# A two-layer decoder step on one Trainium2 core: input sums moved to GpSimd, one top-k search done by bits, output weights split earlier, modulation steps placed later

## The chip, the cores and the metric

The kernel runs as one program on one core of a Trainium2 chip. The core has a matrix engine (TensorE, PE in the rows), VectorE (DVE), ScalarE (ACT), GpSimd (POOL) and SyncE (SP), which issues nearly all the DMAs. The metric is the device time of one execution in microseconds, lower is better. The kernel before takes 2554.56 us, the median of three runs (2552.93 to 2556.01).

## The reference, cut to what matters

The model has two layers, 1024 prompt tokens and 8 sample tokens, a width of 1024, everything in float32. Each sub-layer modulates its input by a shift and a scale that come from a conditioning vector (adaLN), mixes, and ends with `LayerNorm(ALPHA*x + (1+gate)*y)`.

- The modulation of a layer is `silu(c) @ w_ada + b_ada`, cut into six parts of 1024: shift, scale and gate of the mixer, then shift, scale and gate of the channel mixer.
- Layer 0 mixes with a spatial gating unit (SGU): `z = gelu(h @ w_in + b_in)`, halves u and v, v normalised and mixed over chunks of 128 tokens, then `(u * mixed) @ w_out`.
- Layer 1 mixes with sparse attention: an indexer scores all keys for each query, the top 256 of them (128 for a sample token) are kept, and softmax attention runs over those.
- Both layers end with a ConvGLU: `a, u = split(h @ w_up)`, a causal depthwise convolution of width 3 over a, and `(gelu(conv) * u) @ w_down`, with 2816 inner columns.

## The kernel before, in words

**Numbers and tiles.** Activations lie transposed: 128 features on the partitions, tokens along the row, in three chunks of 384, 384 and 264 tokens. Every float32 operand of a large product is split into a high part and a rest (`split`, L111: the high part is a rounded copy, the rest a subtraction, L118), and each product is three matmuls (`mm3`, L98). A piece of weights is 512 KB: SP loads it into one of three `raw` buffers, then its high part (`whi`, L115) and its rest (`wlo`, L118) are written by the engines that `eng` names, GpSimd for both in most places, into tiles of a pool: `W` (4 buffers), `T` (13), `P` (2) or `E` (2).

**The order of the work.** The text of the program gives a priority. A planner then places the instructions of every engine by its own estimate of durations and by the free buffers, and each engine runs in the order that came out. In the loop over the last 18 of 22 ConvGLU tiles (`seven_tile`, L855) the order of TensorE is pinned to that of the text. A queue `fq` holds small steps of other work; `pump(n)` emits the next n of them between two products.

**The SGU stage (up to about 400 us).** `zload(i)` (L341) fetches piece i: 0 to 7 for v, 8 to 15 for u, 16 to 23 the columns of `sgu_w_out`. The loop over u (L630) computes one piece per turn for three chunks, multiplies u into the mixed v (`product`, L626), and in its last turn splits the products into the operand `Hh`, `Hl`. Each turn loads the piece two turns ahead; pieces 18 to 23 are loaded after the loop. `ada_round(0, 2, rawmk)` (L245) is queued after turn 11: eight steps of two 512 KB loads of `w_ada` into `raw` buffers and four matmuls, and an end that turns the sums into shift, scale and gate of the channel mixer. After the loop `gates` and `affine` (L360) prepare the small vectors, and `out_proj` (L669) multiplies: chunk by chunk, for eight pieces, `dense` (L168) and then `accumulate` (L657; L661 on VectorE adds the product into R). Behind each chunk the steps of its LayerNorm (`ln_steps`, L431) are queued: three that normalise (their row tiles come from the pools that `tags` names), and eight that write the next operand with the vectors of `affine`.

**The ConvGLU (about 400 to 1145 us and 1790 to 2500 us).** Inner columns are tiles of 128. Tiles 0 to 3 run in full; from tile `S0` = 4 on, Strassen's scheme does a tile in seven half products. That scheme needs sums of parts of the input (`form_steps`, L781): `sums(k)` makes three rows t1, t2, t4 for each of four k, `parts_of` splits them into tiles `F`, and `third(k)` writes a difference of parts back into `Hh`, `Hl` after tile 3 has used them. These twelve steps are emitted one by one during tiles 2 and 3. The products of the second half (`down`, L709) are queued in `dq` and go to PSUM and then, by L661, into R. In layer 0 each Strassen tile also emits one step of the next layer's modulation (`slow`, L904).

**The top-k search (about 1280 to 1565 us).** For each block of 128 queries the 256th largest score is found bit by bit (`search`, L1216): 31 rounds, in each of which one pass counts the scores above a candidate (L1229 on VectorE) and a few one-column instructions update the candidate. The plan (L39) has VectorE search blocks 2 and 4 together, then block 7 alone (`V2`); ScalarE does the others. The rounds are spread between the heads of the attention.

Of the kernel before, what the change touches and what calls it, by code (L numbers as in the profile page):

```python
# [10 lines left out]
I32 = mybir.dt.int32  # L11
BF = mybir.dt.bfloat16
AF = mybir.ActivationFunctionType
OP = mybir.AluOpType
# [6 lines left out]
T = NPT + NB  # L21
# [31 lines left out]
S0 = 4  # L53
# [7 lines left out]
def hybrid_step(  # L61
# [95 lines left out]
    fq = deque()  # L157

    def pump(n=1):
        for _ in range(n):  # L160
            if fq:
                fq.popleft()()
# [131 lines left out]
    R = newR("R")  # L294
# [44 lines left out]
    pieces = {}  # L339

    def zload(i):  # L341
        if i < 16:
            m = zorder[i]
            pieces[i] = load_w(win[:, m * 128:(m + 1) * 128], 128, eng="AV" if i < 2 else "GG")
        elif i < 24:
            dt = i - 16
            pieces[i] = load_w(sgu_w_out[0][:, dt * 128:(dt + 1) * 128], 128, pool=[None, None, "T", "T", "T", "T", "T", "T"][dt])

# [281 lines left out]
    for i in range(8, 16):  # L630
        m = i - 8
# [11 lines left out]
        if i == 11:  # L643
            drain()
            for c in range(3):
                for k in range(4):
                    product(k, c)
            fq.extend(ada_round(0, 2, rawmk))
        zload(i + 2)
    drain()  # L650
    for i in range(18, 24):
        zload(i)
# [16 lines left out]
    def out_proj(pcs, R, gate, af):  # L669
        for c in range(3):  # L670
            for dt in range(8):
                b = dense(pcs[dt], 128, c)
                accumulate(R, dt, c, b, gate)
                pump(2)
            fq.extend(ln_steps(R, c, af))

    af = affine(0, 3, 0)
    out_proj([pieces[16 + d] for d in range(8)], R, gate, af)


    def conv_glu(l, R, gate, tail_af, last, slow, prefetch=None):
# [99 lines left out]
        def form_steps():  # L781
# [5 lines left out]
            def sums(k):  # L787
# [5 lines left out]
                V.tensor_tensor(t1, t1, x11[1], op=OP.subtract)  # L793
                V.tensor_tensor(t2, x22[0], t1, op=OP.subtract)
                V.tensor_tensor(t2, t2, x22[1], op=OP.add)
                G.tensor_tensor(t4, x21[0], t2, op=OP.subtract)
# [6 lines left out]
            def third(k):  # L803
                x12, x22 = X(0, 1, k), X(1, 1, k)
                d = sm.tile([128, 384], F32, name="d", tag="ht", bufs=2)[:, :TH]
                V.tensor_tensor(d, x22[0], x12[0], op=OP.subtract)
                V.tensor_tensor(d, d, x22[1], op=OP.add)
                V.tensor_tensor(d, d, x12[1], op=OP.subtract)
                split(Hh[:, k, TH:2 * TH], Hl[:, k, TH:2 * TH], d, "A", "V")
# [45 lines left out]
        def seven_tile(ff):  # L855
# [47 lines left out]
            operand(ff, "S4")  # L903
            times = slow.popleft()(True) if slow else None  # L904

# [142 lines left out]
    xsp = [dram.tile([128, KT, CH[c][1]], F32, name=f"xsp{c}") for c in range(3)]  # L1048
    af_box = {}

    spilled = []

    def spill(c):
        SP.dma_start(xsp[c], R[c])
        spilled.append(c)

    class Lazy:
        def __iter__(self):
            if "v" not in af_box:
                af_box["v"] = affine(1, 0, 1)  # L1060
            return iter(af_box["v"])

# [9 lines left out]

    conv_glu(0, R, gate, Lazy(), spill, slow, lambda: (dload(0), dload(1)))

# [141 lines left out]
    def search(name, items, eng):  # L1216
# [9 lines left out]
        if eng == "V":  # L1226
            def counts(c):
                for i, (_, x, n, W, K) in enumerate(items):
# [15 lines left out]
            V.tensor_tensor(cand, cand, bit(30), op=OP.bitwise_or)  # L1244
            V.tensor_scalar(acc, s, 2.0, None, op0=OP.add)
            V.tensor_tensor(tab, pows.unsqueeze(2).to_broadcast([128, 31, m]), acc.unsqueeze(1).to_broadcast([128, 31, m]),
                            op=OP.mult)
            V.tensor_scalar(tab[:, 0, :], tab[:, 0, :], -0.5, None, op0=OP.add)
            V.tensor_scalar(sg, s, 2.0, None, op0=OP.mult)
            for i in range(30, -1, -1):  # L1250
                yield counts(cand)
# [533 lines left out]
```

## Time and profile before

| | |
|---|---|
| median of three runs | 2554.56 us (2552.93 to 2556.01) |
| the profiled execution's own time | 2547.5 us |
| its span, first to last instruction | 2545.8 us |
| TensorE busy in the span | 2450.0 us |
| VectorE / GpSimd / ScalarE busy | 1741.6 / 1376.0 / 985.9 us |
| mean granted TensorE clock | 0.983 |

The profile is of one execution. TensorE is busy for nearly all of the span, so the places to read are those where it waits, and those where its granted clock is below 1. The clock column is in parts of full speed, so a stretch of n us at 0.95 has lost 0.05 n of full-speed time.

### The profile page before, as it was taken

How to read it: one execution, taken by the hardware profiler on the slowest of the kernel's cores; microseconds unless marked ns; L12 is line 12 of the kernel's file. 1: busy time of each engine (PE TensorE's matmuls, PEld its weight loads, DVE VectorE, ACT ScalarE, POOL GpSimd, SP SyncE). 2: the span in 40 equal slices, each digit the busy share in tenths (PEclk: the TensorE clock that was granted, in tenths of full speed). 3: DMA queues.
4: the chain of work that ended last, by engine and by line, in shares of the span. 5: the costliest groups of instructions: out<-in, count | busy, mean ns of one | idle time of the engine just before them, and what ended most of it. 6: DMA issues, size and time to landing. Idle time of an engine off the chain costs nothing.

```text
span 2545.8 us, 41058 instructions
## 1 busy us (share of the span) xinstructions
PE 2450.0 (96%) x15552; PEld 2299.4 (90%) x15552; DVE 1741.6 (68%) x3872; ACT 985.9 (39%) x1906; POOL 1376.0 (54%) x1406
## 2 busy tenths in 40 slices
PE   7999999999999999999999989898999999999997
PEld 5898799789999999998987988777999999999997
DVE  4224335777777777865798997434688888888867
ACT  3121224123333333344567876542423333333341
POOL 3333525436666666574345766533635666666675
PEclk8999999999999999999999999999999999999998
DMA  8413402422222222211114211234111111111112
GB/s 282 124 55 108 125 17 72 131 64 83 81 77 61 81 83 83 82 49 52 62 35 113 54 54 64 63 117 120 59 42 42 50 50 50 47 48 49 50 56 80
DMA packets 203980, 192.14 MB, mean 75 GB/s; under 512 B 9806, under 2 KB 178246, under 8 KB 202999
## 3 DMA queue, kind: packets, MB, share of 16 engines
q1 hardware_dynamic: 200582, 179.86, 22.9%
q0 software_dynamic: 2688, 9.44, 1.2%
q8 instruction: 123, 2.02, 0.3%
q14 instruction: 74, 0.61, 0.1%
q10 hardware_dynamic: 513, 0.23, 0.0%
HBM read 178.41 MB, written 11.27 MB: 75 GB/s over the span
## 4 chain that ended last, share of the span: by engine, by line
PE 78%; DVE 11%; POOL 3%; ACT 3%; issue 2%; DMA 2%; POOLq 0%; SPq 0%; DVEq 0%; ACTq 0%
PE psA L852 28%; PE psB L96 23%; PE psA L96 20%; PE psB L197 3%; PE psB L260 2%; DVE junk L1229 2%; DVE R L661 1%; PE psA L197 1%; DVE S L1209 1%; ACT junk L1260 1%; DMA raw<-in_dsa_w_out_dram 1%; DVE Cc L753 1%; ACT Hh L392 0%; DMA adaw<-in_w_ada_dram 0%; DVE L L1534 0%
## 5 line engine op out<-in xcount | busy, mean ns | idle before, releaser
L661 DVE SCALAR_TENSOR_TENSOR R<-psB,g,R 128x384 f32<-128x384 f32 (+1 forms) x976 | 528.9, 566 | 182.5 <-PE psB L96 181.8
L852 PE MATMUL psA<-Hh,ws 128*128 128x344 f32 x2304 | 578.0, 320 | 0.0
L852 PEld LDWEIGHTS psA<-Hh,ws 128*128 128x128 f32 x2304 | 403.5, 188 | 12.6 <-issue 12.6
L96 PE MATMUL psA<-Hh,whi 128*128 128x384 f32 (+1 forms) x1168 | 381.7, 328 | 13.6 <-POOL whi L115 8.2
L96 PE MATMUL psA<-Hh,wlo 128*128 128x384 f32 (+1 forms) x1168 | 378.6, 325 | 1.2 <-DVE wlo L118 1.2
L96 PE MATMUL psA<-Hl,whi 128*128 128x384 f32 (+1 forms) x1168 | 379.1, 325 | 0.3 <-POOL Hl L398 0.3
L852 PE MATMUL psA<-Hl,ws 128*128 128x344 f32 x1152 | 367.6, 319 | 0.0
L96 PE MATMUL psB<-gh,whi 128*128 128x384 f32 (+1 forms) x1056 | 342.1, 324 | 9.5 <-DVE R L661 7.5
L96 PE MATMUL psB<-gl,whi 128*128 128x384 f32 (+1 forms) x1056 | 338.8, 321 | 0.1
L96 PE MATMUL psB<-gh,wlo 128*128 128x384 f32 (+1 forms) x1056 | 337.2, 320 | 1.4 <-POOL wlo L118 1.4
L118 POOL TENSOR_TENSOR ws<-raw,ws 128x512 fp32r<-128x512 f32 x152 | 201.4, 1327 | 240.1 <-ACT ws L113 240.1
L118 POOL TENSOR_TENSOR wlo<-raw,whi 128x1024 fp32r<-128x1024 f32 (+1 forms) x91 | 232.8, 2560 | 66.7 <-ACT gh L113 48.4
L96 PEld LDWEIGHTS psA<-Hh,whi 128*128 128x128 f32 x1168 | 223.2, 191 | 35.7 <-issue 12.5
L96 PEld LDWEIGHTS psA<-Hl,whi 128*128 128x128 f32 x1168 | 223.2, 191 | 9.8 <-issue 8.6
L96 PEld LDWEIGHTS psA<-Hh,wlo 128*128 128x128 f32 x1168 | 222.9, 191 | 10.0 <-issue 6.7
L118 POOL TENSOR_TENSOR ws<-sf,ws 128x512 fp32r<-128x512 f32 x136 | 176.3, 1302 | 85.5 <-ACT ws L113 74.6
L852 PE MATMUL psA<-F,ws 128*128 128x344 f32 x1296 | 221.9, 320 | 0.0
L852 PEld LDWEIGHTS psA<-Hl,ws 128*128 128x128 f32 x1152 | 216.2, 188 | 0.0
L96 PEld LDWEIGHTS psB<-gh,whi 128*128 128x128 f32 x1056 | 199.0, 188 | 18.1 <-DVE R L661 11.7
L852 PEld LDWEIGHTS psA<-F,ws 128*128 128x128 f32 x1296 | 207.8, 188 | 0.0
L96 PEld LDWEIGHTS psB<-gh,wlo 128*128 128x128 f32 x1056 | 198.9, 188 | 1.7 <-POOL wlo L118 1.7
L96 PEld LDWEIGHTS psB<-gl,whi 128*128 128x128 f32 x1056 | 199.1, 189 | 0.8 <-DVE gl L118 0.8
(419 smaller groups left out, 4730.1 us busy)
## 6 DMA issues: line engine op xcount, KB each, us to landing
raw<-in_ffn_w_up_dram SPq DMA_DIRECT2D x88, 512.0 KB
raw<-in_w_ada_dram SPq DMA_DIRECT2D x64, 512.0 KB
raw<-in_ffn_w_down_dram SPq DMA_DIRECT2D x44, 512.0 KB
adaw<-in_w_ada_dram SPq DMA_DIRECT2D x32, 512.0 KB
raw<-in_sgu_w_in_dram SPq DMA_DIRECT2D x16, 512.0 KB
raw<-in_dsa_w_in_dram SPq DMA_DIRECT2D x16, 512.0 KB
raw<-in_dsa_w_out_dram SPq DMA_DIRECT2D x32, 256.0 KB
raw<-in_sgu_w_out_dram SPq DMA_DIRECT2D x8, 512.0 KB
```

The lines of the kernel that those rows point to most:

```text
L96: pinned(PE.matmul(out, l, r, start=start, stop=stop))
L118: (V if e_lo == "V" else G).tensor_tensor(lo, src, f(hi), op=OP.subtract)
L197: PE.transpose(out, in_, ident[:in_.shape[0], :in_.shape[0]])
L260: pinned(PE.matmul(st["b"][32 * g:32 * g + 32, :512], SCT[:, k, :], rw[g // 2][:, (g % 2) * 512:(g % 2 + 1) * 512], start=(k == 0), stop=( ...
L661: V.scalar_tensor_tensor(R[c][:, dt, :npr], b[:, :npr], gp[:, dt:dt + 1], R[c][:, dt, :npr], op0=OP.mult, op1=OP.add)
L753: V.scalar_tensor_tensor(Cc[:, a0:c0 + npr], As[:, a0 - d:c0 + npr - d], w, Cc[:, a0:c0 + npr], op0=OP.mult, op1=OP.add)
L852: pinned(PE.matmul(b[:, :TH], w[i][:, k, :], x[j], start=first and k == 0 and n == 0, stop=last and k == 3 and n == 2, skip_group_check=True))
L1209: V.scalar_tensor_tensor(S(b)[:, s:s + n], rl[:, :n], WI[:, b, h:h + 1], S(b)[:, s:s + n], op0=OP.mult, op1=OP.add)
L1229: V.tensor_scalar(junkV[:n, :W], x, c if c == 0.0 else f(c[:n, i:i + 1]), 0.0, op0=OP.is_ge, op1=OP.add, accum_out=cnt[:n, i:i + 1])
L1260: A.activation(junkA[:n, :W], x, AF.Sign, bias=c if c == 0.0 else f(c[:n, i:i + 1]), scale=scale if scale == -1.0 else scale[:n, i:i + 1], ...
```

## The change

- **Output pieces of the SGU.** Pieces 16 and 17 are loaded after turns 11 and 12 of the loop over u, piece 18 after turn 14. Piece 16 goes to pool `T`, piece 17 to `E`, piece 18 to `W`; pieces 19 to 23 stay behind the loop and in `T`.
- **Modulation, first seam.** `ada_round(0, 2)` is queued just before `out_proj`; its nine steps go out at one per product from the fifth of chunk 0, then two per product. `affine(0, 3, 0)` is made when its vectors are first used (`Lazy`). The row tiles of the LayerNorm of chunks 0 and 1 come from `P`.
- **Modulation, second seam.** The first Strassen tile of layer 0 emits no step of the next layer's modulation; the rest follow one tile later each.
- **Input sums.** In `sums` the two instructions that make t2, and in `third` all three, run on GpSimd in place of VectorE: 20 instructions in each layer.
- **Search.** The search of block 7 alone keeps a table of bit patterns; a round has two one-column instructions behind the count in place of three.

```diff
@@ zload
-            pieces[i] = load_w(..., 128, pool=[None, None, "T", "T", "T", "T", "T", "T"][dt])
+            pieces[i] = load_w(..., 128, pool=["T", "E", None, "T", "T", "T", "T", "T"][dt])
@@ loop over u
                     product(k, c)
-            fq.extend(ada_round(0, 2, rawmk))
-        zload(i + 2)
+        if i < 14:
+            zload(i + 2)
+        if i in (11, 12, 14):
+            zload({11: 16, 12: 17, 14: 18}[i])
     drain()
-    for i in range(18, 24):
+    for i in range(19, 24):
         zload(i)
@@ out_proj
                 accumulate(R, dt, c, b, gate)
-                pump(2)
-            fq.extend(ln_steps(R, c, af))
-
-    af = affine(0, 3, 0)
-    out_proj([pieces[16 + d] for d in range(8)], R, gate, af)
+                pump(2 if c else int(dt > 3))
+            fq.extend(ln_steps(R, c, af, tags="PP" if c < 2 else "EP"))
+
+    class Lazy:
+        def __init__(self, *args):
+            self.args, self.v = args, None
+        def __iter__(self):
+            if self.v is None:
+                self.v = affine(*self.args)
+            return iter(self.v)
+
+    fq.extend(ada_round(0, 2, rawmk))
+    out_proj([pieces[16 + d] for d in range(8)], R, gate, Lazy(0, 3, 0))
@@ form_steps: sums
-                V.tensor_tensor(t2, x22[0], t1, op=OP.subtract)
-                V.tensor_tensor(t2, t2, x22[1], op=OP.add)
+                G.tensor_tensor(t2, x22[0], t1, op=OP.subtract)
+                G.tensor_tensor(t2, t2, x22[1], op=OP.add)
@@ form_steps: third
-                V.tensor_tensor(d, x22[0], x12[0], op=OP.subtract)
-                V.tensor_tensor(d, d, x22[1], op=OP.add)
-                V.tensor_tensor(d, d, x12[1], op=OP.subtract)
+                G.tensor_tensor(d, x22[0], x12[0], op=OP.subtract)
+                G.tensor_tensor(d, d, x22[1], op=OP.add)
+                G.tensor_tensor(d, d, x12[1], op=OP.subtract)
@@ seven_tile
-            times = slow.popleft()(True) if slow else None
+            times = slow.popleft()(True) if slow and ff > S0 else None
@@ search
+            if m == 1:
+                tab = tab[:, :, 0].bitcast(I32)
+                V.tensor_scalar(bs, cnt, K - 0.5, -1.0, op0=OP.is_ge, op1=OP.mult)
+                V.tensor_tensor(tab, bits, bs.to_broadcast([128, 31]), op=OP.bitwise_and)
+                V.tensor_tensor(tab[:, 1:31], tab[:, 1:31], bits[:, 0:30], op=OP.bitwise_xor)
+                for i in range(30, -1, -1):
+                    yield counts(cand)
+                    V.tensor_scalar(bs, cnt, K - 0.5, float(1 << i), op0=OP.is_gt, op1=OP.mult)
+                    V.scalar_tensor_tensor(cand, bs, tab[:, i:i + 1], cand, op0=OP.bitwise_xor, op1=OP.bitwise_xor)
+            else:
...
-            for i in range(30, -1, -1):
+            for i in range(30, -1, -1) if m > 1 else ():
                 yield counts(cand)
                 V.scalar_tensor_tensor(acc, cnt, K - 0.5, sg, op0=OP.is_gt, op1=OP.mult)
                 V.scalar_tensor_tensor(bs, acc, -0.5 * (1 << i), tab[:, i, :], op0=OP.mult, op1=OP.add)
```

## Rows read from the trace of the kernel before

**Rows 1.** The page's busy times (us, share of the span, instructions) by engine.

```profile
PE 2450.0 (96%) x15552; PEld 2299.4 (90%) x15552; DVE 1741.6 (68%) x3872; ACT 985.9 (39%) x1906; POOL 1376.0 (54%) x1406
```

**Rows 2.** The page's chain that ended last, shares of the span by engine.

```profile
PE 78%; DVE 11%; POOL 3%; ACT 3%; issue 2%; DMA 2%; POOLq 0%; SPq 0%; DVEq 0%; ACTq 0%
```

**Rows 3.** Busy time by stretch: length, engines (instructions), granted clock, DMA share, GB/s.

```profile
289.00:304.00 15.00, 9.65 (x45) 9.33 (x44) 8.21 (x17) 3.17 (x9) 15.00 (x6) 0.77 0.21 62
310.00:398.00 88.00, 88.00 (x597) 87.77 (x596) 28.41 (x58) 24.08 (x39) 34.63 (x41) 1.00 0.09 25
534.00:570.00 36.00, 31.75 (x184) 28.59 (x184) 33.04 (x73) 10.75 (x21) 16.15 (x11) 0.95 0.20 61
573.00:1139.00 566.00, 565.22 (x3596) 547.44 (x3595) 434.18 (x890) 198.13 (x370) 357.46 (x260) 1.00 0.26 77
1387.00:1521.00 134.00, 124.49 (x809) 119.61 (x808) 128.91 (x379) 109.44 (x264) 87.59 (x212) 0.95 0.19 54
1845.00:1892.00 47.00, 42.12 (x248) 40.61 (x247) 46.09 (x84) 11.31 (x23) 19.42 (x15) 0.96 0.12 36
```

**Rows 4.** Timeline of TensorE, 295 to 304 us: start, duration, instruction, idle before.

```profile
299.14 0.69 PE L96 MATMUL psA<-Hh,whi 128*128 128x384 f32 x1 [5.35 <-POOL whi L115]
...
301.23 0.52 PE L96 MATMUL psA<-Hl,whi 128*128 128x384 f32 x1
...
303.67 0.34 PE L96 MATMUL psA<-Hh,whi 128*128 128x384 f32 x1
303.84 0.34 PE L96 MATMUL psA<-Hl,whi 128*128 128x384 f32 x1
```

**Rows 5.** Timeline of GpSimd, 276 to 318 us: the splits of the output pieces.

```profile
288.37 8.52 POOL L118 TENSOR_TENSOR wlo<-raw,whi 128x1024 fp32r<-128x1024 f32 x1
296.86 2.23 POOL L115 TENSOR_SCALAR whi<-raw 128x1024 fp32r<-128x1024 f32 x2
...
314.23 1.05 POOL L115 TENSOR_SCALAR whi<-raw 128x1024 fp32r<-128x1024 f32 x1
315.36 2.42 POOL L118 TENSOR_TENSOR wlo<-raw,whi 128x1024 fp32r<-128x1024 f32 x1
```

**Rows 6.** Timeline of SP's DMA queue, 250 to 320 us.

```profile
261.64 8.66 SPq L252 DMA_DIRECT2D raw<-in_w_ada_dram  x4
274.41 33.26 SPq L124 DMA_DIRECT2D raw<-in_sgu_w_out_dram  x8
```

**Rows 7.** The modulation's line L260: duration ns min/median/max, first and last start.

```profile
L260 PE MATMUL psB<-raw,SCT x256: 592/605/617, 230.3 to 1074.5; 128*32 128x512 f32 x128
```

**Rows 8.** TensorE's waits in 534 to 570 us, then in 1845 to 1892 us.

```profile
PE psB L96 <- DVE R L661: 3.6, 3, 3.0
...
PE psB L96 <- DVE R L661: 3.5, 3, 2.0
```

**Rows 9.** VectorE's groups, 534 to 570 us by form: busy us, mean ns.

```profile
L808 DVE TENSOR_TENSOR d<-d,Hl 128x344 f32<-128x344 f32 x2 | 1.8, 883 | 0.0
...
L806 DVE TENSOR_TENSOR d<-Hh 128x344 f32<-128x344 f32 x2 | 0.9, 502 | 0.0
```

**Rows 10.** VectorE's groups in 1845 to 1892 us, the same columns.

```profile
L661 DVE SCALAR_TENSOR_TENSOR R<-psB,g,R 128x384 f32<-128x384 f32 (+1 forms) x31 | 17.1, 570 | 0.0
...
L793 DVE TENSOR_TENSOR raw<-raw,Hl 128x344 f32<-128x344 f32 x4 | 4.9, 1236 | 0.0
...
L795 DVE TENSOR_TENSOR raw<-raw,Hl 128x344 f32<-128x344 f32 x4 | 2.5, 628 | 0.0
```

**Rows 11.** Line L797, the last sum of an input on GpSimd, both layers.

```profile
L797 POOL TENSOR_TENSOR raw<-raw,Hl x8: 922/962/1287, 469.8 to 1892.5; 128x344 f32<-128x344 f32 x8
```

**Rows 12.** VectorE's groups in 1380 to 1620 us: the search's one-column instructions.

```profile
L1252 DVE SCALAR_TENSOR_TENSOR boxV<-boxV 128x1 f32<-128x1 f32 (+1 forms) x41 | 11.0, 269 | 0.2
L1253 DVE SCALAR_TENSOR_TENSOR boxV<-boxV,misc 128x1 int32<-128x1 f32 x31 | 10.3, 333 | 0.2
L1254 DVE TENSOR_TENSOR boxV<-boxV 128x1 int32<-128x1 int32 (+1 forms) x41 | 10.0, 251 | 0.5
```

More of the change, by code (lines that the diff above doesn't have):

```diff
@@ L346, in zload @@
             dt = i - 16
-            pieces[i] = load_w(sgu_w_out[0][:, dt * 128:(dt + 1) * 128], 128, pool=[None, None, "T", "T", "T", "T", "T", "T"][dt])
+            pieces[i] = load_w(sgu_w_out[0][:, dt * 128:(dt + 1) * 128], 128, pool=["T", "E", None, "T", "T", "T", "T", "T"][dt])
     def mod(L, i):
@@ L1048, in hybrid_step @@
     xsp = [dram.tile([128, KT, CH[c][1]], F32, name=f"xsp{c}") for c in range(3)]
-    af_box = {}
     spilled = []
@@ L1055, in spill @@
         spilled.append(c)
[L1057 to L1061, printed above, removed]
     dwin = dsa_w_in[0]
@@ L1071, in dload @@
             pcs[i] = load_w(dwin[:, o:o + n], n, [None, None, "T", "T", "P"][i] if i < 5 else None, eng=QE if i >= 9 else "GG")
-    conv_glu(0, R, gate, Lazy(), spill, slow, lambda: (dload(0), dload(1)))
+    conv_glu(0, R, gate, Lazy(1, 0, 1), spill, slow, lambda: (dload(0), dload(1)))
     misc = Tt("misc")
@@ L1244, in search @@
             V.tensor_tensor(cand, cand, bit(30), op=OP.bitwise_or)
[L1245 to L1249, printed above, removed]
-            for i in range(30, -1, -1):
+            if m == 1:
[8 more added lines that the diff above has]
+            else:
+                V.tensor_scalar(acc, s, 2.0, None, op0=OP.add)
+                V.tensor_tensor(tab, pows.unsqueeze(2).to_broadcast([128, 31, m]), acc.unsqueeze(1).to_broadcast([128, 31, m]),
+                                op=OP.mult)
+                V.tensor_scalar(tab[:, 0, :], tab[:, 0, :], -0.5, None, op0=OP.add)
+                V.tensor_scalar(sg, s, 2.0, None, op0=OP.mult)
+            for i in range(30, -1, -1) if m > 1 else ():
                 yield counts(cand)
```

## The prediction

> **What bounds the kernel now.** I read the busy times of the page first: TensorE works 2450.0 us of the 2545.8 us span, VectorE 1741.6 [rows 1]. The chain of waits says the same: 78% of it is TensorE, and VectorE comes next with 11% [rows 2]. So time can only come from where TensorE idles or runs at a lower clock, and the busy times by stretch show where the change touches such a place [rows 3]: 289 to 304 us, where the SGU's output projection begins; 534 to 570 and 1845 to 1892 us, where the ConvGLUs of the two layers make the Strassen inputs; 1387 to 1521 us, where block 7 is searched beside the attention. In the last three VectorE is busy 33.0 of 36, 46.1 of 47 and 128.9 of 134 us: there it is VectorE that sets the pace.
>
> **Part 1, the output pieces.** Between 289 and 304 us TensorE idles 15 - 9.65 = 5.35 us, all of it before 299.14, where it waits for a high part from GpSimd [rows 3, 4]. GpSimd was held up: one rest took 8.52 us where a later one takes 2.42, and the next high parts start at 296.86 [rows 5]. All eight pieces are fetched only from 274.41 on, behind the 16 loads of the modulation, the last four of which go out from 261.64 [rows 6]. Piece 17 has moreover to wait for buffers of `W`: four, two per piece, held by pieces 14 and 15 until their products are done. After the wait the matmuls run at the lower clock level (1.2 of 2.4 GHz), with 0.52 in place of 0.34 us each; the 14 from 299.14 to 303.67 take 4.53 us, and at 0.17 from start to start would take 2.4 [rows 4]: 2.1 us lost. With pieces 16 to 18 split during the loop over u, the first three products (24 matmuls of 0.17, 4.1 us each) are covered. The other five pieces cost GpSimd 1.05 + 2.42 = 3.5 us each [rows 5], less than a product, and have 12 us of lead, minus what the last v tiles take to leave pool `T`. I count **-5.35 - 2.1 = -7.5 us**; worth nothing if piece 19 is late instead.
>
> **Part 2, the modulation in the output projection.** Nothing is added or dropped: eight steps of two loads and four matmuls (L260, 0.6 us each [rows 7]), one end with a copy, four transposes and four sums, and the ten small instructions of `affine` move behind the start of the projection. On SP its 16 loads now stand behind the output pieces, ahead of the ConvGLU's first weights. At 8.66 / 4 = 2.2 us each [rows 6] they take 35 us, from about 17 us into the projection (five pieces at 3.5 us must leave the `raw` buffers first): done some 52 us in. The projection takes about 109 us (289 to 398, without a gap from 310 on [rows 3]), so over 50 us are left for the LayerNorm steps of two chunks and the first weights. I count 0; without that cover each us of lateness is a us. Chunk 0's and 1's row tiles both in `P` cost nothing either: chunk 1's steps stand behind chunk 0's in the queue.
> The step left out of the first Strassen tile is also 0: from 573 to 1139 us TensorE works 565.2 of 566 us [rows 3], each later step goes out one tile later, and the last matmul of them at 1074.5 [rows 7] leaves room for one more tile.
>
> **Part 3, the input sums.** Per layer 8 instructions of `sums` and 12 of `third` go from VectorE to GpSimd. A sum of this shape takes 0.50 us on VectorE where nothing disturbs it [rows 9] and 0.96 on GpSimd [rows 11]. Layer 0: TensorE idles 36 - 31.75 = 4.2 us, 3.6 of it for VectorE's additions into R, the longest 3.0 [rows 3, 8], and loses 0.05 x 36 = 1.8 us to the clock. Two of the four `third` run in that stretch: 0.9 + 0.9 + 1.8 = 3.6 us [rows 9], L807, which has no row, at the price of L806. Gain between -6.0 (all of idle and clock) and, if VectorE is blocked for all the six instructions' time on GpSimd, 6 x 0.96 - 3.6 = +2.2. I take **-3**, the relief less a fifth, as VectorE is nearly full. Layer 1: idle 4.9, clock 0.04 x 47 = 1.9 [rows 3]; three waits for VectorE make 3.5 [rows 8]. Here the eight t2 instructions lie in the stretch: 8 x 0.63 = 5.0 us of VectorE [rows 10]. Ends -6.8 and 8 x 0.96 - 5.0 = +2.7; I take **-3**, less than the relief, since VectorE keeps the slow ones. GpSimd has room: 16 of 36 and 19 of 47 us busy [rows 3].
>
> **Part 4, the search.** 31 rounds lose one of three one-column instructions, whose means here are 0.27, 0.33 and 0.25 us [rows 12]: 31 x 0.25 = 7.8 us off VectorE. The new forms (a compare that writes an integer, a double xor) are in no row; the nearest are the integer lines L1253 and L1254 [rows 12], and I price them alike. TensorE has 9.5 us idle and 0.05 x 134 = 6.7 us of lost clock in the stretch [rows 3]. Ends: 0 if a round stays as long, -10.3 at 0.33 us a round. I take half of 7.8, **-4**, because ScalarE (109 of 134 us) holds up the heads too. The table's set-up is three instructions for four: 0.
>
> **Sum.** -7.5 - 3 - 3 - 4 = -17.5. The profiled execution took 2547.5 us (span 2545.8), 7 us under the median, so it would come to 2530; against the median of 2554.6 it is **2537**.
>
> **Rivals.**
> *Only the first seam pays.* VectorE's relief is swallowed by the next wait in the same stretch (ScalarE's activations, or the additions that then bunch up). For it: VectorE stays nearly full in all three stretches. Against: the waits name its additions. 2554.6 - 7.5 = 2547.
> *The modulation is late.* In chunk 1 two steps go with each product: 4 loads of 2.2 us against 4.1 us of matmuls. If the planner, which thinks in estimates, keeps that order, the last four steps cost 2 x (8.7 - 4.1) = 9.2 us and a clock drop of 2.1: -17.5 + 11.3, 2548. Against: the loads of 261.64 kept up at one step per product.
> *The change doesn't do what it says.* The planner may split pieces 16 to 18 no earlier, or the wait comes back at pieces 19 to 23, which need `T` buffers that v holds to the end, and GpSimd's sums cost what VectorE saves: 2554, no change.
> *GpSimd blocks VectorE (slower).* Place: tiles 2 and 3 of both ConvGLUs. In 1845 to 1892 us L793, with two inputs in SBUF, takes 1.24 us, while L661, with one input in PSUM, stays at 0.57 [rows 10]; so some of VectorE's instructions seem to wait for GpSimd's. If all the time of 20 sums on GpSimd, 19.2 us a layer, blocks a VectorE that gives off only 20 x 0.50, each layer pays +9.2: 18.4 - 7.5 - 4 = +6.9, 2561. It decides once VectorE has less idle time than it is blocked for; in layer 1 that is 0.9 us of 47 [rows 3]. Against: the 31 additions that share the stretch are not stretched, and 12 of the 20 need not fall there.
> The Trainium skill has this as a rule (SBUF — State Buffer, "Who interferes with whom"): a VectorE instruction with two SBUF inputs and a GpSimd one that reads SBUF share a port pair, which the first holds to its end. By it the moved sums block for longer than they relieve. The trace agrees in the pair L793 and L661.
>
> **Chances and range.** Forecast 0.55; only the first seam 0.18; late modulation 0.09; no effect 0.09; blocked 0.09. A measurement of this kernel tells about 0.2% (5 us) from no change. Faster: 0.55, 0.13 of the second, 0.08 of the third: 0.76. Slower: the last, 0.09; same 0.15. The forecast's own range is 2530 to 2545 (the four ends together, -30.6 and -2.6, are unlikely). The range goes up to 2552 to take in the second and third cases, down to 2527 for a search that pays in full.
>
> **What would show it.** Right: no wait of TensorE for `whi` at the first output products and a clock of 1.00 there; shorter waits for L661 near 560 and 1850 us; two one-column lines in the rounds of block 7 and less VectorE time from 1387 us on. Wrong: a wait for `w_ada` loads inside the projection or for `Hh` at the first ConvGLU product; L118 and L753 longer beside the new GpSimd sums; the search's stretch as long as before.

## The result and the profile after

| | before | after |
|---|---|---|
| median of the runs (us) | 2553.96 (2550.07 to 2556.01, 6 runs) | 2539.16 (2535.93 to 2541.47, 6 runs) |
| ratio after to before | | 0.9943, 95% interval 0.9933 to 0.9953 |
| profiled execution: run, span (us) | 2547.5, 2545.8 | 2541.47, 2539.8 |

The change gains 14.8 us; 2537 was forecast. The spans of the two profiles differ by only 6.0 us, since the execution of before was shorter than every timed run of that kernel, and the one of after was the longest of its six. Stretches are therefore compared below over more than one profile.

The page of after, its busy times and its chain, which answer to [rows 1, 2]:

```profile
PE 2451.6 (97%) x15552; PEld 2297.8 (90%) x15552; DVE 1731.7 (68%) x3800; ACT 986.1 (39%) x1906; POOL 1416.3 (56%) x1446
...
PE 79%; DVE 9%; POOL 4%; ACT 3%; issue 2%; DMA 2%; SPq 0%; POOLq 0%; DVEq 0%; ACTq 0%
```

VectorE has 72 instructions and 10 us less, GpSimd 40 instructions and 40 us more. VectorE's share of the chain fell from 11% to 9%. The busy times by stretch of after, columns as in [rows 3], each stretch set where the same work now lies:

```profile
272.00:306.00 34.00, 34.00 (x196) 30.74 (x195) 12.47 (x27) 6.48 (x17) 16.42 (x8) 1.00 0.41 127
303.80:391.80 88.00, 88.00 (x562) 74.74 (x562) 25.94 (x64) 22.15 (x35) 21.43 (x32) 1.00 0.26 79
529.00:565.00 36.00, 34.10 (x208) 30.88 (x208) 31.90 (x69) 10.86 (x22) 19.92 (x16) 1.00 0.19 59
568.00:1134.00 566.00, 564.03 (x3589) 546.36 (x3588) 430.42 (x885) 197.06 (x368) 362.43 (x262) 1.00 0.26 77
1378.00:1512.00 134.00, 122.25 (x785) 116.19 (x785) 128.85 (x356) 107.07 (x260) 88.07 (x209) 0.95 0.19 52
1839.00:1886.00 47.00, 43.42 (x266) 41.32 (x265) 45.37 (x72) 10.79 (x21) 32.42 (x25) 1.00 0.14 42
```

Line by line against [rows 3]: where the output projection begins (about 289.4 us before, 273.6 in after) TensorE now works 34.00 of 34 us at clock 1.00; before it worked 9.65 of 15 at 0.77. In the form of layer 0 it works 34.10 of 36 (31.75), again at 1.00 (0.95). Around the search nothing got better: 122.25 of 134 us, before 124.49. In the form of layer 1 it works 43.42 of 47 (42.12), at 1.00 (0.96). "Form" is the stretch in which the Strassen inputs are made. The whole way from the SGU's first `U` to the last addition of the output projection, before and then after:

```profile
160.76:398.08 237.32, 231.97 (x1507) 215.09 (x1506) 91.84 (x219) 60.32 (x106) 97.54 (x93) 0.99 0.24 72
```

```profile
163.01:391.84 228.83, 228.83 (x1498) 211.53 (x1497) 93.82 (x218) 57.60 (x101) 88.66 (x89) 1.00 0.24 72
```

TensorE idled 5.35 us there and now doesn't idle at all.

The timeline of GpSimd in after, 236 to 300 us, its splits of weights, and after it SP's queue from 200 us on, which answer to [rows 5, 6]:

```profile
240.33 1.28 POOL L115 TENSOR_SCALAR whi<-raw 128x1024 fp32r<-128x1024 f32 x1
241.70 2.39 POOL L118 TENSOR_TENSOR wlo<-raw,whi 128x1024 fp32r<-128x1024 f32 x1
...
277.37 3.69 POOL L115 TENSOR_SCALAR whi<-raw 128x1024 fp32r<-128x1024 f32 x1 [7.41 <-DVE Hl L118]
...
290.55 1.06 POOL L115 TENSOR_SCALAR whi<-raw 128x1024 fp32r<-128x1024 f32 x1
291.69 2.43 POOL L118 TENSOR_TENSOR wlo<-raw,whi 128x1024 fp32r<-128x1024 f32 x1
```

```profile
240.39 43.61 SPq L124 DMA_DIRECT2D raw<-in_sgu_w_out_dram  x6
...
287.12 44.98 SPq L252 DMA_DIRECT2D raw<-in_w_ada_dram  x16
```

The output pieces are fetched ahead of the modulation's 16 loads, and GpSimd is done with the last one at 294.1, some 20 us into the projection and in time for it. Its wait of 7.41 us ahead of 277.37 is for VectorE's split of the last products; the lead covers it. The longest rest in 236 to 300 us is 2.59 us; the one of 8.52 us is gone. TensorE's waits of after in 529 to 565 us, then in 1839 to 1886 us (who waits on whom: us, times, longest), against [rows 8] (the answers for the two stretches, one under the other):

```profile
PE psB L96 <- DVE R L663: 1.2, 3, 0.6
...
PE psB L96 <- DVE R L663: 2.5, 3, 1.8
```

L663 is the addition into R that was L661. In layer 0 its longest wait went from 3.0 to 0.6 us, in layer 1 only from 2.0 to 1.8.

### The profile page after: what moved, and what is told of

Read it like the earlier page. It is cut to its first block, busy times and chain, and to the rows that moved or that the text cites. A ratio compares the mean times of both kernels' runs of the same rounds, so it can differ in the third digit from the quotient of the medians.

```text
span 2539.8 us, 41011 instructions
## 1 busy us (share of the span) xinstructions
PE 2451.6 (97%) x15552; PEld 2297.8 (90%) x15552; DVE 1731.7 (68%) x3800; ACT 986.1 (39%) x1906; POOL 1416.3 (56%) x1446
## 4 chain that ended last, share of the span: by engine, by line
PE 79%; DVE 9%; POOL 4%; ACT 3%; issue 2%; DMA 2%; SPq 0%; POOLq 0%; DVEq 0%; ACTq 0%
PE psA L865 28%; PE psB L96 22%; PE psA L96 21%; PE psB L197 3%; PE psB L260 2%; ACT junk L1277 1%; DVE junk L1235 1%; DVE S L1215 1%; PE psA L197 1%; DVE R L663 1%; ACT Hh L392 1%; DVE Cc L766 1%; DMA adaw<-in_w_ada_dram 0%; POOL L L1555 0%; POOL wh L115 0%
## 5 line engine op out<-in xcount | busy, mean ns | idle before, releaser
L663 DVE SCALAR_TENSOR_TENSOR R<-psB,g,R 128x384 f32<-128x384 f32 (+1 forms) x976 | 529.6, 567 | 176.8 <-PE psB L96 175.9
L96 PE MATMUL psB<-gl,whi 128*128 128x384 f32 (+1 forms) x1056 | 337.7, 320 | 0.2
L118 POOL TENSOR_TENSOR wlo<-raw,whi 128x1024 fp32r<-128x1024 f32 (+1 forms) x91 | 226.9, 2496 | 63.7 <-ACT gh L113 54.3
L118 DVE TENSOR_TENSOR gl<-Cc,gh 128x344 fp32r<-128x344 f32 (+1 forms) x132 | 200.4, 1521 | 6.0 <-ACT gh L113 5.6
```

What stands on the lines that cost most here:

```text
L96: pinned(PE.matmul(out, l, r, start=start, stop=stop))
L118: (V if e_lo == "V" else G).tensor_tensor(lo, src, f(hi), op=OP.subtract)
L663: V.scalar_tensor_tensor(R[c][:, dt, :npr], b[:, :npr], gp[:, dt:dt + 1], R[c][:, dt, :npr], op0=OP.mult, op1=OP.add)
```

## The experiments

Twelve kernels ran, each with the kernel before beside it on the same chip; one of them (e12) is that kernel itself, profiled once more. "In us" below is the ratio's distance from 1 times 2555. The gains of the parts don't add up, so two tables come first. The first has the runs:

| kernel | what of the change it has | median, before beside it | ratio, 95% interval | in us |
|---|---|---|---|---|
| e5_pieces | early pieces | 2564.72, 2555.98 | 1.0043 (1.0028 to 1.0058) | +11.0 |
| e16_pieces_tags | early pieces, pool P | 2547.66, 2553.57 | 0.9976 (0.9967 to 0.9985) | -6.1 |
| e1_seam | pieces, pool P, modulation moved | 2552.59, 2555.04 | 0.9991 (0.9982 to 1.0001) | -2.3 |
| e2_sums | sums | 2561.05, 2555.04 | 1.0020 (1.0011 to 1.0028) | +5.1 |
| e9_s0 | no step at S0 | 2551.77, 2553.57 | 0.9990 (0.9977 to 1.0004) | -2.6 |
| e10_sums_s0 | sums, no step at S0 | 2552.54, 2555.98 | 0.9993 (0.9983 to 1.0003) | -1.8 |
| e3_search | search | 2552.93, 2555.04 | 0.9988 (0.9979 to 0.9997) | -3.1 |
| e4_no_search | all but the search | 2543.82, 2555.04 | 0.9957 (0.9943 to 0.9972) | -11.0 |
| e11_no_s0 | all but the missing step | 2549.17, 2555.98 | 0.9977 (0.9967 to 0.9987) | -5.9 |
| e15_no_sums | all but the sums | 2545.55, 2553.57 | 0.9965 (0.9951 to 0.9978) | -8.9 |
| e17_no_move | all but the modulation's move | 2542.52, 2553.18 | 0.9959 (0.9946 to 0.9972) | -10.5 |
| after | all | 2539.16, 2553.96 | 0.9943 (0.9933 to 0.9953) | -14.6 |

The second has the stretches of one profile each (us), cut at the same events in all: from the SGU's first `U` to the last addition of its output projection (**A**), on to the last Strassen product of layer 0 (**B**), to the first score product (**C**), to the last one (**D**), to the first Strassen product of layer 1 (**E**). The letter in E says which order TensorE's instructions have there: equal letters, equal order.

| kernel | A | B | C | D | E |
|---|---|---|---|---|---|
| before | 237.3 | 737.1 | 271.5 | 336.9 | 187.6 x |
| before, again (e12) | 238.1 | 738.8 | 274.8 | 343.9 | 185.6 x |
| e9_s0 | 237.3 | 734.6 | 272.6 | 337.7 | 189.3 x |
| e1_seam | 228.8 | 740.8 | 275.2 | 343.7 | 189.5 x |
| e2_sums | 237.1 | 743.3 | 275.1 | 343.7 | 185.4 w |
| e3_search | 237.0 | 738.2 | 272.2 | 344.1 | 183.2 y |
| e5_pieces | 228.6 | 748.2 | 280.5 | 345.3 | 182.9 y |
| e16_pieces_tags | 231.0 | 739.2 | 274.9 | 343.8 | 183.7 y |
| e15_no_sums | 228.8 | 738.6 | 274.5 | 343.8 | 182.3 y |
| e10_sums_s0 | 237.0 | 733.5 | 274.0 | 344.8 | 181.7 z |
| e4_no_search | 230.3 | 734.9 | 274.0 | 343.6 | 182.5 z |
| e17_no_move | 231.0 | 734.3 | 275.0 | 343.8 | 182.0 z |
| e11_no_s0 | 228.8 | 743.5 | 271.7 | 344.1 | 183.3 v |
| after | 228.8 | 732.8 | 273.6 | 343.2 | 183.8 z |

### The four parts, each by itself or left out

Four kernels take the whole seam (pieces, pool and modulation), the sums and the search alone, and the change without its search.

```
e1_seam:       pool=["T", "E", None, "T", ...]; zload(16..18) inside the loop over u;
               tags="PP" if c < 2 else "EP"; ada_round(0, 2) behind the output pieces; Lazy affine
e2_sums:       V.tensor_tensor -> G.tensor_tensor in t2 (2 of each k) and third (3 of each k)
e3_search:     the branch "if m == 1" of search()
e4_no_search:  the whole change, search() as before
```

> The kernel before with the early output pieces and the modulation moved into the output projection, and nothing else. My theory: the 5.35 us wait for a high part and the 2.1 us of lower clock at the projection's start go, and nothing comes back later: 7.5 us faster, 0.9971 of the time before (6 to 9 us). Rival (late modulation): 4 us slower to 1 us faster, with a wait for loads of w_ada or for Hh between 300 and 400 us. Rival (the wait comes back at pieces 19 to 23): no difference.

> The kernel before with the 20 input sums of each layer on GpSimd, and nothing else. My theory: the waits for L661 near 560 and 1850 us shrink: 6 us faster, 0.9977 (3 to 9 us), about half of it in each layer. Rival (GpSimd blocks VectorE): up to 18 us slower, with two-input VectorE instructions beside the sums longer than before. Rival (relief swallowed): within 2 us, TensorE waiting for something else in the same stretches.

> The kernel before with the search of block 7 by bits, and nothing else. My theory: 4 us faster (0 to 10), 0.9984, between 1387 and 1521 us. Rival, after the profile of the changed kernel (its attention stage came out 6 us longer, with more waits for GpSimd's scaling and a lower clock): VectorE is relieved, but the planner lays the heads and the filling products out anew, and the stage takes as long or longer: 0 to 6 us slower.

> The changed kernel with the old search of block 7. My theory: 4 us slower than the changed kernel, so about 11 us faster than before (0.9957). Rival (the search pays nothing or costs): the same as the changed kernel or up to 6 us faster than it, 15 to 21 us faster than before (0.992 to 0.994).

The seam alone came out 2.3 us lower, where 7.5 were expected, and its interval holds 1. The sums alone made the kernel slower by 5.1. The search alone and the change without the search came out in time as expected; but in e3_search the attention stage D took 344.1 us, which its rival had said and its theory had not. Alone, seam, sums and search give -2.3 + 5.1 - 3.1 = -0.3 us; together with the missing step they give -14.6. So the parts work on each other, and the theory that each is worth its own sum falls.

The seam did its work where it was meant to: A is 228.8 in place of 237.3 and 238.1. Its loss is later: B is 2 to 4 us longer, and E keeps order x.

The sums met something that the prediction had put at 0, the modulation's step at the first Strassen tile. The waits of TensorE in e2_sums, 535 to 1140 us:

```profile
PE psB L260 <- DMA raw<-in_w_ada_dram: 3.6, 1, 3.6
PE psB L96 <- DVE t L665: 1.7, 3, 0.9
PE psB L96 <- DVE R L661: 1.2, 3, 0.6
```

The wait for L661 fell as forecast (3.6 to 1.2 us), but the step now waits 3.6 us for its weights. The timelines say why. First GpSimd before and in e2_sums, then SP's queue before and in e2_sums, then the matmuls of the step (L260) before and in e2_sums:

```profile
560.90 1.54 POOL L833 TENSOR_TENSOR raw<-raw 128x512 f32<-128x512 f32 x1
562.41 1.45 POOL L834 TENSOR_TENSOR raw<-raw 128x512 f32<-128x512 f32 x1
```

```profile
567.50 1.56 POOL L833 TENSOR_TENSOR raw<-raw 128x512 f32<-128x512 f32 x1
569.02 1.29 POOL L834 TENSOR_TENSOR raw<-raw 128x512 f32<-128x512 f32 x1
```

```profile
563.89 5.10 SPq L252 DMA_DIRECT2D raw<-in_w_ada_dram  x2
```

```profile
570.35 4.88 SPq L252 DMA_DIRECT2D raw<-in_w_ada_dram  x2
```

```profile
573.51 1.06 PE L260 MATMUL psB<-raw,SCT 128*32 128x512 f32 x8
```

```profile
574.12 1.05 PE L260 MATMUL psB<-raw,SCT 128*32 128x512 f32 x4
578.74 1.92 PE L260 MATMUL psB<-raw,SCT 128*32 128x512 f32 x4 [3.56 <-DMA raw<-in_w_ada_dram]
```

Six sums of `third`, some 7 us of GpSimd, now stand ahead of L833 and L834, which free the `raw` buffers, and SP's first load of the step goes out 6.5 us later by the clock of the profile. But 4.6 of that is a shift of everything: the first Strassen product starts at 558.95 in place of 554.36. Counted from that product the loads go out only 1.9 and 1.7 us later. The other half is TensorE: with the wait for L661 and the dip behind it gone it reaches the step 15.17 us after that product, in place of 19.15, so it wants the weights 4.0 us sooner. Before, that wait had covered the loads.

Not all that e2_sums lost is this wait. B is 5.3 us longer than the mean of before's two, and 2.3 of that lie ahead of the first Strassen product: e2_sums and e10_sums_s0 take 158.6 us from the last addition of the output projection to there, before 156.3, with the same 1.2 us of idle time and a clock of 1.00. TensorE's instructions lie in another order there, and 1.9 of the 2.3 us stand in the matmuls of L260. What chose that order was not found.

### The sums and the step at S0

```
e10_sums_s0 = e2_sums + "if slow and ff > S0"      e9_s0 = that condition alone
e11_no_s0   = the change with "if slow"            e15_no_sums = the change with V for the 20 sums of a layer
```

> The 20 sums of each form on GpSimd and, with them, no slow step at the product step of the first tile (S0); nothing else of the change. Theory (the sums alone were slower because their GpSimd steps delayed the copies that free the raw buffers, so the w_ada loads for S0 were issued 6.5 us later and TensorE waited 3.56 us for them at 575 us): without a slow step at S0 that wait cannot arise, the relief of the L661 waits near 560 and 1850 us stays, and the Strassen stage of layer 0 takes about 575 us in place of 585 with the sums alone and 581 before; time 2547 to 2551 us. Rival 1 (GpSimd's tensor operations slow VectorE down wherever they stand): still 3 to 6 us slower than before, 2558 to 2561 us. Rival 2 (the parts only pay with the pieces split ahead): no change, 2554 to 2556 us.

> The changed kernel with the slow step of the first tile back in its place: everything else of the change stays. Theory (that step is what the sums on GpSimd collide with): the wait of some 3 to 4 us for raw<-w_ada comes back near 568 us, the layer-0 Strassen stage takes about 579 us in place of 575, time 2543 us. Rival (the step was hidden work in both kernels and its removal is worth nothing): 2539 us with no wait for w_ada near 568 us.

> Only the slow step at the first tile (S0) taken away; the sums stay on VectorE. Theory (the step costs nothing where its loads come in time, as in the kernel before, and is worth something only together with the sums on GpSimd, which make those loads late): 2554 to 2556 us, the wait of 3.0 us on L661 near 562 us stays, the stretch from the last output product to the last Strassen product of layer 0 takes 737 to 739 us as before. Rival (the gain of sums and step together is the step's own): that stretch takes 733 to 735 us, time 2550 to 2552 us.

> The changed kernel with the 40 sums back on VectorE; pieces, modulation, first tile's step and search as changed. Theory (with the step gone the sums on GpSimd are worth the L661 wait near 560 us and the clock's dip behind it, some 5 us, and about nothing in layer 1): 2543 to 2545 us, a wait of 3 us on L663 near 556 us with half clock behind it. Rival 1 (the sums bring nothing, the missing step does): 2539 us or less. Rival 2 (the sums bring the 6 us forecast, half of it in layer 1): 2545 us or more and waits on L663 of over 3 us in the form of layer 1.

The theory that the two collide holds. In the change, with the step put back, B takes 743.5 in place of 732.8, and the wait is there again, first line below (TensorE's waits of e11_no_s0, 535 to 1140 us). Behind it the busy times of the same 21 us, e11_no_s0, then after:

```profile
PE psB L260 <- DMA raw<-in_w_ada_dram: 3.5, 1, 3.5
```

```profile
556.00:577.00 21.00, 17.52 (x87) 14.69 (x88) 9.71 (x20) 4.88 (x10) 10.75 (x10) 0.84 0.35 103
```

```profile
556.60:577.60 21.00, 20.38 (x129) 20.06 (x128) 16.31 (x35) 7.78 (x16) 16.48 (x14) 1.00 0.25 75
```

TensorE idles 3.5 us and then runs at the lower clock (0.84 in the mean, 1.00 in after). In us: sums and no step -14.6, without the sums -8.9, without the missing step -5.9. The sums are worth 5.7 us in the change, where the step is gone; alone, beside the step, they cost 5.1. The step is worth 8.7, mostly since the sums are there. The change without both was not run. The median of e10_sums_s0 lies 1.5 us above its range and its interval holds 1, and e11_no_s0 lies 6 us above its forecast of 2543: the direction was right, the sizes were not.

How much of this the step is worth by itself stays open. By the letter e9_s0 fell to its rival: 2551.77 us and a B of 734.6 lie in the rival's ranges, though the wait of 3.0 us for L661 stayed, as its theory had it. But the kernel before ran at 2553.57 beside it, and its interval holds 1. In B, without the seam, the step alone took off 3.4 us (from 738.0, the mean of before's two), the sums and the step together 4.5; with the seam the step alone took off 2.2 (e1_seam to e15_no_sums) and both 8.0 (e1_seam to after). e15_no_sums took 2545.55 us, half a us above its theory's range and within rival 2's; what tells them apart are the waits. That of 3.1 us for L663 and the dip are back in layer 0, as the theory said; for rival 2 those in layer 1 would have to be over 3 us, and the longest is 1.4.

The pair e15_no_sums and after also shows the sums of each layer by themselves: nothing else in their text differs, though the planner laid out B, C and E in another order. The two form stretches of e15_no_sums (layer 0, layer 1), to be held against the third and sixth line of after above:

```profile
528.60:564.60 36.00, 31.63 (x183) 28.42 (x183) 32.86 (x73) 10.76 (x21) 15.12 (x10) 0.95 0.20 60
1843.20:1890.20 47.00, 43.41 (x268) 41.25 (x267) 46.83 (x84) 11.60 (x23) 24.82 (x17) 1.00 0.13 39
```

In layer 0 TensorE works 34.10 us with the sums on GpSimd and 31.63 without, and the clock's dip is gone: 2.5 + 1.8 = 4.3 us. In layer 1 it works 43.42 and 43.41: nothing. What became of the relief there stands in VectorE's groups by form (busy us, mean ns), e15_no_sums and then after:

```profile
L663 DVE SCALAR_TENSOR_TENSOR R<-psB,g,R 128x384 f32<-128x384 f32 x20 | 11.6, 607 | 0.0
...
L118 DVE TENSOR_TENSOR F<-raw,F 128x1032 fp32r<-128x1032 f32 x3 | 3.7, 1224 | 0.0
L118 DVE TENSOR_TENSOR gl<-Cc,gh 128x264 fp32r<-128x264 f32 x3 | 3.6, 1195 | 0.0
L807 DVE TENSOR_TENSOR raw<-Hh,raw 128x344 f32<-128x344 f32 x4 | 2.6, 660 | 0.1
L808 DVE TENSOR_TENSOR raw<-raw,Hl 128x344 f32<-128x344 f32 x4 | 2.5, 630 | 0.0
```

```profile
L663 DVE SCALAR_TENSOR_TENSOR R<-psB,g,R 128x384 f32<-128x384 f32 x19 | 11.0, 605 | 0.0
L118 DVE TENSOR_TENSOR F<-raw,F 128x1032 fp32r<-128x1032 f32 x3 | 6.2, 2060 | 1.1 <-ACT F L113 1.1
L118 DVE TENSOR_TENSOR gl<-Cc,gh 128x264 fp32r<-128x264 f32 x3 | 5.8, 1934 | 0.0
```

The eight sums that went (L807, L808) were 5.1 us. VectorE's whole busy time in the stretch fell only from 46.83 to 45.37. The splits of `F` and `gl`, which read two inputs from SBUF, grew from 1.22 to 2.06 and from 1.20 to 1.93 us, 4.7 us together. (VectorE's other input sums changed both ways, L806 from 1.53 to 0.50, L805 from 0.51 to 1.15 and L804 from 0.51 to 0.72 us each, 0.6 us less together.) The additions L663, with one input in PSUM, stayed at 0.61. By the Trainium skill (SBUF — State Buffer, "Who interferes with whom") a VectorE instruction with two inputs in SBUF contends with one of GpSimd that reads SBUF, and one with at most one input there, outside the modes that take both port pairs, doesn't. The trace agrees: 0.74 to 0.84 us more on the splits, none on L663.

### The pieces and the layer norm's pool

```
e5_pieces:        pools and early zload only
e16_pieces_tags:  e5_pieces and
-            fq.extend(ln_steps(R, c, af))
+            fq.extend(ln_steps(R, c, af, tags="PP" if c < 2 else "EP"))
```

> Only the output pieces split ahead with their pools; the modulation's steps stay ahead of the output products and the layer norm's tags stay. Theory A (moving the modulation is what gives back most of the seam's gain, by its products in the convolution's stage, where two waits of 0.60 and 0.78 us for R L400 stood, and a clock dip): the seam stage still takes 229 us in place of 237, the following convolution stage 156 us as before in place of 159, time 2547 to 2549 us. Theory B (the modulation's move costs and brings nothing; the rest of the loss is spread over later stages that are laid out anew or vary from one run to the next): as with the whole seam, 2551 to 2553 us. Rival C (the modulation has to move for the pieces to be early: its loads would stand ahead of them on SP): the wait of 5 us at the first output products stays, 2554 to 2556 us.

> Output pieces split ahead with their pools, and the layer norm's tiles of the first two chunks in pool P in place of E and P; the modulation's steps stay where they were. Theory A (the pieces alone lost because piece 17 took the only buffer of pool E, in which the layer norm of the second chunk keeps a normalised block, so the norm came after the last output products): the convolution stage takes 156 to 159 us in place of 166, the wait of 2.45 us for raw L425 near 391 us and the dip behind it go, time 2547 to 2553 us. Theory B (the modulation's move is what the early pieces need): 2562 to 2566 us, as with the pieces alone.

The pieces alone lost 11.0 us, outside what any of the three theories had said: A fell to 228.6, but B rose to 748.2. With the one line for the pool, the same kernel gained 6.1: theory A of the second run holds in time and place, and it is one line that makes the early pieces worth having. The timeline of ScalarE at L425, which writes the normalised blocks of the layer norm, 330 to 404 us in e5_pieces and then in e16_pieces_tags:

```profile
334.77 1.44 ACT L425 ACTIVATE n<-psB,mv 128x512 f32<-128x512 f32 x2 [32.03 <-POOL mv L410]
342.75 1.45 ACT L425 ACTIVATE raw<-psB,mv 128x512 f32<-128x512 f32 x2 [6.54 <-POOL mv L410]
367.18 1.45 ACT L425 ACTIVATE n<-psB,mv 128x512 f32<-128x512 f32 x2 [22.98 <-PE psA L96]
...
392.13 1.45 ACT L425 ACTIVATE raw<-psB,mv 128x512 f32<-128x512 f32 x2 [3.74 <-POOL mv L410]
```

```profile
335.94 2.79 ACT L425 ACTIVATE n<-psB,mv 128x512 f32<-128x512 f32 x4 [31.68 <-POOL mv L410]
343.48 1.45 ACT L425 ACTIVATE raw<-psB,mv 128x512 f32<-128x512 f32 x2 [4.75 <-POOL mv L410]
373.54 2.79 ACT L425 ACTIVATE n<-psB,mv 128x512 f32<-128x512 f32 x4 [13.75 <-POOL mv L410]
380.06 1.45 ACT L425 ACTIVATE raw<-psB,mv 128x512 f32<-128x512 f32 x2 [3.73 <-POOL mv L410]
```

With the pool changed, two blocks are written at 335.94 in one go. In e5_pieces one of them, a block of the first chunk, waits until 367.18, released by a product of TensorE: piece 17 holds both buffers of pool E, its high part and its rest, until the third chunk has used it. The second chunk's last block moves back 12 us, to 392.13, after the last output product. TensorE then waits 2.45 us for L425 at 390.5, and from 391 to 399 us its mean clock is 0.79. The wait on TensorE's timeline of e5_pieces and the busy times of 391 to 399 us:

```profile
392.96 0.69 PE L197 MATMUL psB<-ident,raw 128*128 128x128 f32 x2 [2.45 <-ACT raw L425]
```

```profile
391.00:399.00 8.00, 4.89 (x24) 3.82 (x24) 2.67 (x5) 6.87 (x12) 5.91 (x7) 0.79 0.00 0
```

The two ratios lie 17 us apart, the spans of the two profiles 12.2. Of these, 7.6 stand between the first `U` and the first Strassen product of layer 0, where this wait lies; 5.6 stand in C, which is laid out in another order, and are not explained.

### The modulation's move

```
e17_no_move: the change with ada_round(0, 2) back in the loop over u, affine(0, 3, 0) ahead of out_proj,
             and pump(2) after every product
```

> The changed kernel with the modulation's steps back ahead of the output products and its pump of two steps a product, the layer norm's tiles of the first two chunks kept in pool P (third chunk as before); pieces, sums, first tile's step and search as changed. Theory (early pieces and pool P are all that the seam needs, the modulation's move itself is worth about nothing): 2537 to 2541 us; the seam stage takes 231 us in place of 228.8 and the convolution's and Strassen stretch gives those 2 us back. Rival 1 (the move costs, by the two waits of 0.60 and 0.78 us for R L400 and the dip behind them near 435 us): 2536 us or less. Rival 2 (the move brings something): 2542 us or more.

The run gave 2542.52, by the letter rival 2 (the move brings something). Its ratio, 0.9959 (0.9946 to 0.9972), overlaps that of the change, 0.9943 (0.9933 to 0.9953), so the medians don't settle it. The stretches lean the same way: A and B together are 965.3 us without the move and 961.6 with it. In the change the move is worth between nothing and 4 us. Beside the pieces and the pool alone it went the other way: e16_pieces_tags -6.1, e1_seam -2.3, with intervals that just overlap; there E alone, in order y in the one (183.7) and x in the other (189.5), differs by more. The cost that rival 1 of this run names is there as well: after has two waits for R at L400, of 0.8 and 0.6 us, between 284 and 440 us, and e17_no_move has none. So the sign of the move by itself stays open.

### The kernel before, again

> The kernel before, profiled once more, to see how far one profile stands for it. The profile at hand spans 2545.8 us, some 7 us under the timed runs, and its attention stage (first to last score product) takes 336.9 us where all five other kernels, three of which leave that stage as it was, took 343 to 344. If that was one lucky execution: span 2551 to 2554 us, attention stage 342 to 344 us. If the order of the work in the kernel before makes the stage shorter: 337 us again.

The run took 2558.4 us (one run), with a span of 2556.7 and an attention stage of 343.9 us. So the profile that the prediction rests on was a short execution, and the order of the work alone doesn't make it so, for TensorE's instructions have the same order in both from A to E. The two attention stages, profile of before and then its repeat:

```profile
1406.65:1743.59 336.94, 313.80 (x2085) 277.50 (x2083) 223.48 (x610) 208.73 (x446) 182.56 (x324) 0.97 0.23 71
```

```profile
1413.60:1757.50 343.90, 318.62 (x2084) 281.87 (x2083) 223.97 (x609) 209.65 (x446) 183.07 (x322) 0.96 0.22 69
```

Of the 7.0 us, 25.3 - 23.1 = 2.1 are idle time of TensorE and 4.8 busy time at a lower mean clock. D is 343 to 346 us in every other profile but that of e9_s0 (337.7). That one has the order of before in D, and no profile of another order does; so with this order D was short in two of three executions, with the others in none of eleven. Whether an execution can be short only in this order stays open. Either way D is no stage from which a single pair of profiles can be read to better than 7 us.

## Why the prediction was right, step by step

The time, 2539 against 2537, was right, and so was the mechanism of the largest term. That the sum came so close is in part luck. Of its terms the pieces stand at their size and place, the search at its size but not its place, layer 0's sums at nearly twice their size, layer 1's at 0; the modulation's 0 stands within the error. And two edits priced at 0, the pool and the missing step, decide whether the pieces and the sums gain anything.

- **Part 1, pieces, -7.5.** Right in mechanism and size. The wait of 5.35 us and the low clock behind it are gone, and A is 8.5 to 9.3 us shorter than in the two profiles of before. Some 2 us of that is work moved on: nine transposes of the layer norm stand behind A in after, and where they stay in it (e16_pieces_tags, e17_no_move) A is 6.3 to 7.1 shorter. Pieces 19 to 23 were in time. That it holds alone was wrong: it rests on the pool.
- **Part 2, "Chunk 0's and 1's row tiles both in `P` cost nothing either".** This is the step that failed most. They were looked at as a cost, and cost none, but without them the pieces lose. From e5_pieces to e16_pieces_tags the edit is worth 11.0 + 6.1 = 17 us. Piece 17's buffers in E had another user, the layer norm, which the prediction didn't follow up.
- **Part 2, the modulation, 0.** Within the error in the change (0 to -4); beside the pieces and the pool alone it was +3.8. Its 16 loads went out from 287.12 to 332.1, at 2.8 us each in place of 2.2, and no wait for `w_ada` arose in the projection. The rival of the late modulation is out.
- **Part 2, the step left out of the first tile, 0.** Mis-sized: some 9 us in the change. It was priced against the kernel before, where its loads came in time behind the wait for L661, and not against the kernel with the sums on GpSimd, where the loads go out 1.9 us later and TensorE comes for them 4.0 us sooner.
- **Part 3, layer 0, -3.** 4.3 us in the form's stretch, 5.7 in the whole time, with the step gone; the sign turns where the step stays (+5.1 alone). The relief less a fifth (2.9 us) left out the dip of the clock, 1.8 us, that went with the wait.
- **Part 3, layer 1, -3.** It was 0: the splits gave back what the sums relieved. E is 2 to 4 us shorter than before, but as much so in the four kernels without the sums on GpSimd that have order y (183.0 in the mean, against 182.5 in the four with order z, all with the sums, and 188.0 in the four with x). What chose between x and y was not found.
- **Part 4, search, -4.** The size is right: -3.1 alone, 14.6 - 11.0 = 3.6 in the whole. The rounds also got shorter, but not as worked out. One small instruction of each round (the second in before's second profile, the first and then the second in after), its duration in ns (min/median/max) and its first and last start:

```profile
L1253 DVE SCALAR_TENSOR_TENSOR boxV<-boxV,misc x31: 128/159/2370, 1400.9 to 1527.8; 128x1 int32<-128x1 f32 x31
```

```profile
L1259 DVE TENSOR_SCALAR boxV<-boxV x31: 130/147/155, 1388.0 to 1506.6; 128x1 int32<-128x1 f32 x31
L1260 DVE SCALAR_TENSOR_TENSOR boxV<-boxV,misc x31: 201/220/2455, 1388.2 to 1506.8; 128x1 int32<-128x1 int32 x31
```

  30 rounds went from 126.9 to 118.6 us, 8.3 less (6.3 less than in before's first profile, 1395.0 to 1519.9), against 7.8 forecast for 31. The instructions themselves give less: the means in [rows 12] hold single ones of over 2 us, the medians before are some 0.16 us each, and the double xor takes 0.22 and not the price of its nearest row. That is about 0.11 us a round, 3.3 in all; the rest stands between them. And D is as long with it as without (344.1 and 343.9, 343.2 and 343.6). The one stretch of e3_search's profile that is more than 1 us shorter than in both profiles of before is E, in order y. So that the gain comes from the search's own chain is not shown; and in the whole change the intervals with and without it overlap.
- **Rivals.** *Only the first seam pays* named the right fate of layer 1's sums, but not of layer 0's. *GpSimd blocks VectorE* has its mechanism (splits at 2.06 in place of 1.22 us in layer 1) and not its end: what VectorE lost was about as much as it gave off, not more. The slower time of the sums alone came in part from the step's wait for its loads and in part from another order of TensorE's work.
- **The base.** The profile's 7 us under the median were kept as a constant between the two, and the time was forecast from the median. That was the right base: the repeat of the same kernel came out 10.9 us longer in its span, so the 7 us are nothing that the kernel has in every execution.

## What to carry to other kernels

When work moves to another engine, follow what that engine does next for the transfers: a few microseconds of sums ahead of the instructions that free a load's buffer made the load late, just as the relief brought TensorE to it sooner, and the gain was lost until the step that needed the load was taken away. When a tile goes into another pool, look for every other user of that pool's buffers within its lifetime: one tag was worth more than the edit that it served. Measure parts both alone and left out, and profile the kernel before twice, before a stage is blamed.

## What the runs showed of the hardware that was not expected

- Two executions with the same order of TensorE's instructions differed by 7.0 us in one stage of 340 us, at a mean granted clock of 0.97 and 0.96, and by 10.9 us in the span.
- In the form of layer 0 the granted clock fell to its lower level (1.2 of 2.4 GHz) behind the wait of 3.0 us (mean 0.95 in 36 us, before and in e15_no_sums); in after, with 0.6 us in its place, it stayed at 1.00. The clock gave back 1.8 us on top of the wait's 2.4.
- In the form of layer 1 VectorE's splits with two inputs in SBUF took 0.74 to 0.84 us more each with the sums on GpSimd (after) than without (e15_no_sums), a little less than the length of one sum on GpSimd (0.96 us [rows 11]).
